# Two-block transformer step on one core: the first normalisation moved behind the transposes, column sums by transposes, gates and two key products column by column, other slots for the loads

## The chip, the cores and the metric

One core of one Trainium2 chip runs one program on 256 tokens of width 1024. The metric is the device time of one execution in microseconds (us); the number that counts is the median of several runs. The engines are PE (TensorE, matmuls and transposes), DVE (VectorE), ACT (ScalarE), POOL (GpSimd) and SP (SyncE, which here only issues the weight loads). Each executes its own instructions in the order in which they stand in its queue.

## The reference, cut to what matters

Two blocks follow each other. The first one is all that the change touches:

```python
mod = silu(c) @ w_ada + b_ada                      # 6 vectors of 1024: sh_m, sc_m, gt_m, sh_f, sc_f, gt_f
h = rmsnorm(x, norm_mix_g) * (1 + sc_m) + sh_m
q, k, v, f_logit, u = split(h @ w_in)              # 512, 512, 512, 8, 512 columns
log_f = log_sigmoid(f_logit + b_fgate)             # forget gates, 8 heads; F = cumsum(log_f)
x = x + gt_m * (concat(forgetting_attention(q, k, v, log_f), multiscale_pool(u)) @ w_out)
h = rmsnorm(x, norm_ffn_g) * (1 + sc_f) + sh_f
x = x + gt_f * hierarchical_moe(h)                 # 32 experts, 2 per token, 96 MB of weights
x = rmsnorm(x, norm_final_g)
# second block: stick-breaking attention, HGRN2, merge, square-ReLU MLP
```

## The kernel before, in words

All weights are streamed from HBM in tiles of 1 MB (128 x 2048 floats) by SP, in one fixed order, each into a numbered slot of SBUF (`Stream`, from L26; the issue is L51). SP issues a load when the slot's last tenant has been read, and a load that waits holds back all loads behind it. In the first part there are 11 slots (0 to 10). The order and the slots stand in the table `plan`: `a0` to `a7` are the eight tiles of `w_ada` that give sh_m and sc_m, `b` and `c` the other sixteen, `i0` and `i1` the keys' weights, `i2` and `i3` the values', `i4` to `i7` pairs of query and pool features, `o0` to `o3` `w_out`. Behind them come the 96 expert tiles (`w_gu`, `w_dn`), whose slots are those of the list `slots` and five extra ones: 18 tiles can lie ready before the first is read.

Products with `w_in` are made in three passes: a half tile of weights is split into a rounded part `whi` (ACT, L70) and a remainder `wlo` (DVE, L71), the activations are split likewise into `hT` and `hL`, and `mmx` (L140 to L142) issues hi x hi, hi x lo and lo x hi. `next2` takes the next split half and has the following ones split ahead, three halves at most.

The front runs in this order. (1) The rows of x get their norm: squares on ACT (L251), `r1` on DVE (L252, L243 to L245), and both halves are scaled (L257 on DVE, L259 on ACT). (2) PE transposes the scaled rows (L274) to eight columns of features, `xT[0..7]`. (3) For each column d of 128 features, `ada_first` makes the modulation: eight products of tile `a_d` with silu(c) (L292) in four strips of PSUM, a copy to `mr` (ACT, L294), and two one-column matmuls with ones that add the strips up (L298); it makes the products of column d+1 before the sums of column d. DVE adds the bias (L299) and forms A1 (L359). (4) `evac_split` turns column d into `hT` and `hL`: even columns DVE (L351), ACT (L352), POOL (L353), odd columns ACT (L344), DVE (L345, L346). (5) With all columns done: 24 small matmuls for the forget gates (`pf`), their log-sigmoid on ACT (L378 to L382) and cumulative sum on DVE (L383 to L389), then four key products (`feat`, 24 matmuls each), the values, and in turn queries, attention scores and pooling; single steps of the other modulation tiles (`some`, L311 to L325) lie between. `w_out`, the router and the experts follow, and then the second block.

Of the kernel before, what the change touches and what calls it, by code (L numbers as in the profile page):

```python
# [14 lines left out]
OP = mybir.AluOpType  # L15
# [102 lines left out]
LOOK, LOOK3 = 2, 3  # L118
SOME = (1, 1, 1, 1, 1, 3, 2, 2)
# [3 lines left out]
def body(tc, nc, ctx, a, out):  # L123
# [56 lines left out]
    st.slots.update({i: (ring if i < 4 else ring2, f"w{i}") for i in range(11)})  # L180

    st.slots.update({15: (hp_, "hT"), 16: (hp_, "hL")})
    plan = "a0-7 0-7 i0-4 0-4 b0-3 5-8 i5 9 b4 10 b5 5 i6 6 b6-7 7-8 c0 0 i7 1 c1-2 2-3 o0 8 c3 10 c4 5 c5 7 o1 0 c6 4 c7 2 o2 3 o3 10"
    src = {"a": (a["w_ada"][0], 0), "b": (a["w_ada"][1], 0), "c": (a["w_ada"][2], 0), "i": (a["w_in"], 1), "o": (a["w_out"], 1)}

    def span(x):
        lo, _, hi = x.partition("-")
        return range(int(lo), int(hi or lo) + 1)

    plan = plan.split()  # L190
    for what, where in zip(plan[::2], plan[1::2]):
        w, split = src[what[0]]
        for i, slot in zip(span(what[1:]), span(where)):
            st.add(w[i], split, slot)
# [60 lines left out]
    def scale_rows(dst, src, r, t):  # L255
        if t == 0:
            V.tensor_scalar(dst[:, t], src[:, t], r[:, t:t + 1], None, op0=OP.mult)  # L257
        else:
            S.activation(dst[:, t], src[:, t], AF.Copy, scale=r[:, t:t + 1])  # L259

    xn = cp.tile([128, 2, 1024], F32, name="xn")
    r1 = q1.tile([128, 2], F32, name="r1")
    rms_scale(r1, xt, q1, xn)
    for t in range(2):
        scale_rows(xn, xt, r1, t)
# [12 lines left out]
    xT = transposed(ps, "a", xn)  # L278
# [4 lines left out]
    def ada_first():  # L283

        last = None
        for d in range(9):
            if d < 8:
                w = st.next()
                pa = ps.tile([128, 512], F32, name="pa", tag="m", bufs=2)
                for k in (0, 2, 4, 6, 1, 3, 5, 7):  # L290
                    j = 32 * (k // 2)
                    mm(pa[j:j + 32, 0:256], cs[:, k, :], w[:, 256 * k:256 * k + 256], start=(k % 2 == 0), stop=(k % 2 == 1))  # L292
                mr = q1.tile([128, 256], F32, name="mr", bufs=2)
                S.activation(mr, pa[:, 0:256], AF.Copy)  # L294
            if last:
                pl, ml = last
                for j in range(2):
                    mm(pl[:, 256 + j:257 + j], ml[:, 128 * j:128 * j + 128], ones, start=True, stop=True)  # L298
                V.tensor_tensor(modT[:, 0:2, d - 1], pl[:, 256:258], vec[:, V_BA + d - 1:V_BA + 16:8], op=OP.add)  # L299
                yield  # L300
            last = pa, mr
# [27 lines left out]
    def mod(m):  # L329
        return modT[:, m]  # L330
# [72 lines left out]
    for i in range(4):  # L403
        feat(st.next2(), kT[:, i])
# [40 lines left out]
    scr = q1.tile([128, 2048], F32, name="scr", tag="scr")  # L445
# [251 lines left out]
    slots = [9, 15, 16, 5, 7, 2, 1, 0, 3, 6, 4, 8, 10]  # L697
# [1084 lines left out]
```

## Time and profile before

| what | us |
|---|---|
| three runs | 750.92, 746.55, 751.06 (median 750.92) |
| the profiled execution, its own time | 746.88 |
| its span, first to last instruction | 745.1 |
| mean granted TensorE clock in it | 0.967 |
| PE busy | 681.0 (91% of the span) |
| DVE, ACT, POOL busy | 398.4, 303.8, 139.9 |

Busy shares are means over parts with different limits: to about 151 us the front with its attention and router, from there to about 350 us the experts, then the second block. Starts are in us from the span's start. A matmul's row shows its whole passage through the array; how often one is started is read from the distance of the starts.

### The profile page before, as it was taken

The numbers are of one execution on the slowest core, as the hardware profiler recorded it, in microseconds if no ns is written. First come the engines' busy times: TensorE is split into PE (matmuls) and PEld (weight loads), VectorE is DVE, ScalarE is ACT, GpSimd is POOL, SyncE is SP. The second block draws the span as 40 slices with busy tenths as digits, with TensorE's granted clock in tenths as the row PEclk, the third lists the DMA queues.
The fourth block names the chain that finished last, engine by engine and source line by source line (L and its number), as shares of the span: only waits on it lengthen the run. The fifth ranks groups of instructions, "written<-read, shape, count | busy, mean of one in ns | idle before, by whom it ended". The sixth has DMA issues, their size and how long they took to land.

```text
span 745.1 us, 12246 instructions
## 1 busy us (share of the span) xinstructions
PE 681.0 (91%) x4953; PEld 525.2 (70%) x4953; DVE 398.4 (53%) x661; ACT 303.8 (41%) x531; POOL 139.9 (19%) x137
## 2 busy tenths in 40 slices
PE   3899999889799877877899999999999999999995
PEld 2598867644244313311799999999989998989885
DVE  2676896522122112011888877777867654545545
ACT  3544534321011001001585566586456654535433
POOL 0102521000000000000604342222413530503201
PEclk9999999999889889789999999999999999999998
DMA  9999499999999999999664333355446655455511
GB/s 362 418 420 408 192 408 420 419 384 421 419 420 420 421 421 421 421 422 421 253 211 169 131 114 113 115 191 205 170 170 206 218 175 219 172 186 207 173 58 56
DMA packets 29726, 207.70 MB, mean 279 GB/s; under 512 B 3553, under 2 KB 3937, under 8 KB 4706
## 3 DMA queue, kind: packets, MB, share of 16 engines
q1 hardware_dynamic: 29520, 206.35, 70.3%
q8 instruction: 41, 0.67, 0.4%
q10 hardware_dynamic: 146, 0.53, 0.2%
q14 instruction: 19, 0.16, 0.1%
HBM read 205.81 MB, written 1.05 MB: 278 GB/s over the span
## 4 chain that ended last, share of the span: by engine, by line
PE 52%; DMA 16%; DVE 3%; ACT 1%; issue 1%; DVEq 0%; ACTq 0%; SPq 0%
DMA w<-in_w_gu 11%; PE pp L140 9%; PE pp L141 9%; PE pp L142 9%; DMA w<-in_w_dn 5%; PE fy L142 4%; PE fy L141 4%; PE fy L140 4%; PE pB L1265 2%; PE y L847 1%; PE pv L140 1%; PE pv L141 1%; PE pv L142 1%; PE acc L141 1%; PE acc L140 1%; PE acc L142 1%
## 5 line engine op out<-in xcount | busy, mean ns | idle before, releaser
L71 DVE TENSOR_TENSOR wlo<-w,whi 128x1024 fp32r<-128x1024 f32 x144 | 182.0, 1267 | 98.0 <-ACT whi L70 97.7
L70 ACT ACTIVATE whi<-w 128x1024 fp32r<-128x1024 f32 x146 | 153.4, 1054 | 78.5 <-PE fy L142 39.7
L141 PE MATMUL pp<-hL,whi 128*128 128x256 f32 x368 | 102.9, 280 | 2.6 <-DVE hL L876 2.6
L140 PE MATMUL pp<-hT,whi 128*128 128x256 f32 x368 | 105.1, 286 | 0.0
L142 PE MATMUL pp<-hT,wlo 128*128 128x256 f32 x368 | 103.1, 280 | 0.5 <-DVE wlo L71 0.5
L930 PE MATMUL pgu<-w,hg 128*32 128x512 f32 x512 | 70.3, 665 | 20.3 <-DMA w<-in_w_gu 20.2
L140 PEld LDWEIGHTS pp<-hT,whi 128*128 128x128 f32 x368 | 70.0, 190 | 3.5 <-issue 2.4
L141 PEld LDWEIGHTS pp<-hL,whi 128*128 128x128 f32 x368 | 69.7, 189 | 2.8 <-POOL wlo L71 2.7
L140 PE MATMUL pp<-nH,whi 128*128 128x256 f32 x256 | 71.5, 279 | 0.0
L141 PE MATMUL pp<-nL,whi 128*128 128x256 f32 x256 | 71.3, 279 | 0.0
L142 PE MATMUL pp<-nH,wlo 128*128 128x256 f32 x256 | 71.3, 279 | 0.0
L142 PEld LDWEIGHTS pp<-hT,wlo 128*128 128x128 f32 x368 | 70.0, 190 | 0.7 <-DVE wlo L71 0.7
L930 PEld LDWEIGHTS pgu<-w,hg 128*32 128x32 f32 x512 | 14.2, 113 | 71.4 <-issue 46.8
L1544 POOL TENSOR_TENSOR aL<-rs,aH 128x256 fp32r<-128x256 f32 x32 | 46.1, 1442 | 86.7 <-ACT aH L1543 80.8
L934 DVE TENSOR_TENSOR act<-pgu,act 128x256 f32<-128x256 f32 x8 | 3.4, 425 | 104.4 <-ACT act L933 104.4
L933 ACT ACTIVATE act<-pgu 128x256 f32<-128x256 f32 x8 | 3.1, 383 | 127.8 <-PE pgu L930 127.8
L142 PEld LDWEIGHTS pp<-nH,wlo 128*128 128x128 f32 x256 | 48.6, 190 | 0.0
L141 PE MATMUL fy<-wlo,aH 128*128 128x512 f32 x124 | 48.2, 389 | 0.0
L142 PE MATMUL fy<-whi,aL 128*128 128x512 f32 x124 | 48.2, 389 | 0.0
L140 PE MATMUL fy<-whi,aH 128*128 128x512 f32 x124 | 48.2, 389 | 0.0
L141 PEld LDWEIGHTS pp<-nL,whi 128*128 128x128 f32 x256 | 48.1, 188 | 0.1
L140 PEld LDWEIGHTS pp<-nH,whi 128*128 128x128 f32 x256 | 48.1, 188 | 0.1
(430 smaller groups left out, 1286.7 us busy)
## 6 DMA issues: line engine op xcount, KB each, us to landing
w<-in_w_gu SPq DMA_DIRECT2D x64, 1024.0 KB, 19.8
w<-in_w_dn SPq DMA_DIRECT2D x32, 1024.0 KB, 19.8
w<-in_w_ff SPq DMA_DIRECT2D x32, 1024.0 KB, 4.8
w<-in_w_in SPq DMA_DIRECT2D x30, 1024.0 KB, 5.9
w<-in_w_ada SPq DMA_DIRECT2D x24, 1024.0 KB, 12.5
w<-in_w_out SPq DMA_DIRECT2D x8, 1024.0 KB, 4.8
w<-in_w_o SPq DMA_DIRECT2D x4, 1024.0 KB, 4.8
xt<-in_x SPq DMA_DIRECT2D x1, 1024.0 KB, 4.8
```

Source lines behind the costliest of these rows:

```text
L70: nc.scalar.activation(hi, w, AF.Copy)
L71: low = lambda e, lo=lo, w=w, hi=hi: e.tensor_tensor(lo, w, hi.bitcast(F32), op=OP.subtract)
L140: mm(out_, l[0], r[0], start=start, stop=False)
L141: mm(out_, l[0], r[1], start=False, stop=False)
L142: mm(out_, l[1], r[0], start=False, stop=stop)
L847: mm(pacc[t][h], pw[g][:, 128 * t:128 * t + 128], o, start=False, stop=(g == 7))
L930: mm(pgu[32 * j:32 * j + 32], hg[g][:, k, 32 * j:32 * j + 32], w[:, 512 * j:512 * j + 512], start=(k == 0), stop=(k == 7))
L933: S.activation(act, pgu[:, 0:256], AF.Silu)
L934: V.tensor_tensor(act, pgu[:, 256:512], act, op=OP.mult)
L1265: mm(p[:, 4 * t + h], kt[:, h, 128 * t:128 * t + 128], qo[:, h, n * t:n * t + n], start=True, stop=True)
L1544: G.tensor_tensor(aL[:, f], s, aH[:, f].bitcast(F32), op=OP.subtract)
```

## The change

Seven edits, all in the front, and the slots of later loads:

1. The rows are transposed raw (`transposed(ps, "a", xt)`), before the norm. The factor `r1` is brought across all partitions by a matmul: a diagonal matrix `dg1` (DVE, two instructions) times a matrix of ones, copied out as `rb1` (ACT). The scaling of the rows (L257, L259) is gone.
2. The strip sums of a column come from two transposes and a DVE reduction over every 32nd column of the result; the bias is added in an instruction of its own.
3. A column leaves PSUM in one form for all d: DVE multiplies by A1 and `rb1` (`evt`), ACT adds the shift and rounds (`hT`), DVE forms the remainder (`hL`). POOL has no part in it.
4. The sums of column d now stand in the program before the products of column d+1.
5. From column 3 on, between the products and the sums of column d, PE makes the matmuls of column d-2 for two key products and for the gates (nine); tile `i0` is split before that, behind column 2.
6. The splits of `i1` come after column 7; the copies of the first two key products (`kT`) come behind the gates' log-sigmoid.
7. `plan` loads `i0` between `a2` and `a3`, `i1` behind `a7`, and gives other slots; so do `slots` and `RING`, from which the second block's weights are loaded.

```diff
+RING = (4, 5, 7, 1)
...
-    plan = "a0-7 0-7 i0-4 0-4 b0-3 5-8 i5 9 b4 10 b5 5 i6 6 b6-7 7-8 c0 0 i7 1 c1-2 2-3 o0 8 c3 10 c4 5 c5 7 o1 0 c6 4 c7 2 o2 3 o3 10"
+    plan = """a0:0 a1:1 a2:2 i0:3 a3:4 a4:5 a5:6 a6:7 a7:8 i1:9 i2:10 i3:0 i4:1 b0:2 b1:3 b2:4 b3:5 i5:6 b4:7 b5:8 i6:9 b6:10 b7:2
+        c0:3 i7:0 c1:4 c2:5 o0:1 c3:7 c4:6 c5:8 o1:10 c6:9 c7:2 o2:0 o3:3"""
-    plan = plan.split()
...
-        if t == 0:
-            V.tensor_scalar(dst[:, t], src[:, t], r[:, t:t + 1], None, op0=OP.mult)
-        else:
-            S.activation(dst[:, t], src[:, t], AF.Copy, scale=r[:, t:t + 1])
-    r1 = q1.tile([128, 2], F32, name="r1")
-    rms_scale(r1, xt, q1, xn)
-    for t in range(2):
-        scale_rows(xn, xt, r1, t)
+    scr = q1.tile([128, 2048], F32, name="scr", tag="scr")
+    full = scr[:, 0:128]
+    G.memset(full, 1.0)
...
-    xT = transposed(ps, "a", xn)
+    xT = transposed(ps, "a", xt)
+    r1 = q1.tile([128, 2], F32, name="r1")
+    rms_scale(r1, xt, q1, xn)
+    dg1, rb1 = scr[:, 128:384], scr[:, 384:640]
+    for t in range(2):
+        V.tensor_scalar(dg1[:, 128 * t:128 * t + 128], ident, r1[:, t:t + 1], None, op0=OP.mult)
+    def row_scales():
+        p = ps.tile([128, 256], F32, name="prb1", tag="s", bufs=2)
+        mm(p, full, dg1, start=True, stop=True)
+        S.activation(rb1, p, AF.Copy)
-    def ada_first():
-        last = None
-        for d in range(9):
-            if d < 8:
-                w = st.next()
-                pa = ps.tile([128, 512], F32, name="pa", tag="m", bufs=2)
-                for k in (0, 2, 4, 6, 1, 3, 5, 7):
-                    j = 32 * (k // 2)
-                    mm(pa[j:j + 32, 0:256], cs[:, k, :], w[:, 256 * k:256 * k + 256], start=(k % 2 == 0), stop=(k % 2 == 1))
-                mr = q1.tile([128, 256], F32, name="mr", bufs=2)
-                S.activation(mr, pa[:, 0:256], AF.Copy)
-            if last:
-                pl, ml = last
-                for j in range(2):
-                    mm(pl[:, 256 + j:257 + j], ml[:, 128 * j:128 * j + 128], ones, start=True, stop=True)
-                V.tensor_tensor(modT[:, 0:2, d - 1], pl[:, 256:258], vec[:, V_BA + d - 1:V_BA + 16:8], op=OP.add)
-                yield
-            last = pa, mr
+    pas = {}
+    def ada_products(d):
+        w = st.next()
+        pa = ps.tile([128, 512], F32, name="pa", tag="m", bufs=2)
+        for k in (0, 2, 4, 6, 1, 3, 5, 7):
+            j = 32 * (k // 2)
+            mm(pa[j:j + 32, 0:256], cs[:, k, :], w[:, 256 * k:256 * k + 256], start=(k % 2 == 0), stop=(k % 2 == 1))
+        mr = q1.tile([128, 256], F32, name="mr", bufs=2)
+        S.activation(mr, pa[:, 0:256], AF.Copy)
+        pas[d] = pa, mr
+    def ada_sums(d):
+        pa, mr = pas.pop(d)
+        p = pa[:, 256:512].rearrange("p (j c) -> p j c", j=2)
+        for j in range(2):
+            nc.tensor.transpose(p[:, j], mr[:, 128 * j:128 * j + 128], ident)
+        m = modT[:, 0:2, d]
+        V.tensor_reduce(m, p[:, :, 0:128:32], axis=AX.X, op=OP.add)
+        V.tensor_tensor(m, m, vec[:, V_BA + d:V_BA + 16:8], op=OP.add)
+        V.scalar_tensor_tensor(A1[:, d:d + 1], mod(1)[:, d:d + 1], 1.0, vec[:, V_GM + d:V_GM + d + 1], op0=OP.add, op1=OP.mult)
+        e = q1.tile([128, 256], F32, name="evt", bufs=3)
+        V.scalar_tensor_tensor(e, xT[d], A1[:, d:d + 1], rb1, op0=OP.mult, op1=OP.mult)
+        sh = mod(0)[:, d:d + 1]
+        S.activation(hT[:, d], e, AF.Identity, bias=sh)
+        V.scalar_tensor_tensor(hL[:, d], e, sh, hT[:, d].bitcast(F32), op0=OP.add, op1=OP.subtract)
...
-    for d, _ in enumerate(ada_first()):
-        V.scalar_tensor_tensor(A1[:, d:d + 1], mod(1)[:, d:d + 1], 1.0, vec[:, V_GM + d:V_GM + d + 1], op0=OP.add, op1=OP.mult)
-        evac_split(q1, xT[d], hT[:, d], hL[:, d], A1[:, d:d + 1], mod(0)[:, d:d + 1], v=d % 2)
-    st.split_to(LOOK)
+    pf, early = [], []
+    def gate_column(k):
+        if not pf:
+            pf.append(ps.tile([128, 256], F32, name="pf", tag="s", bufs=2))
+        mmx(pf[0][0:8], (wfh[:, k], wfl[:, k]), (hT[:, k], hL[:, k]), start=(k == 0), stop=(k == 7))
+    def key_column(k):
+        if not early:
+            early.extend((ps.tile([128, 256], F32, name="pp", tag=tag, bufs=n), st.next2(False)) for tag, n in (("a", 4), ("s", 2)))
+        for p, w in early:
+            mmx(p, sub(w, slice(None), slice(128 * k, 128 * k + 128)), (hT[:, k], hL[:, k]), start=(k == 0), stop=(k == 7))
+    ada_products(0)
+    row_scales()
+    ada_sums(0)
+    for d in (1, 2):
+        ada_products(d)
+        ada_sums(d)
+    gate_column(0)
+    st.split_to(2)
+    key_column(0)
+    for d in range(3, 8):
+        ada_products(d)
+        key_column(d - 2)
+        gate_column(d - 2)
+        ada_sums(d)
+    for k in (6, 7):
+        key_column(k)
+        gate_column(k)
+    st.split_to(1)
     nc.sync.dma_start(wpl, a["w_pool"])
     nc.sync.dma_start(wr, a["w_r"])
...
-    pf = ps.tile([128, 256], F32, name="pf", tag="a", bufs=4)
-    for k in range(8):
-        mmx(pf[0:8], (wfh[:, k], wfl[:, k]), (hT[:, k], hL[:, k]), start=(k == 0), stop=(k == 7))
-    S.activation(fz, pf[0:8], AF.Identity, bias=vec[0:8, V_BF:V_BF + 1])
+    S.activation(fz, pf[0][0:8], AF.Identity, bias=vec[0:8, V_BF:V_BF + 1])
...
     for i in range(4):
-        feat(st.next2(), kT[:, i])
+        if i < 2:
+            S.activation(kT[:, i], early[i][0], AF.Copy)
+        else:
+            feat(st.next2(), kT[:, i])
...
-    slots = [9, 15, 16, 5, 7, 2, 1, 0, 3, 6, 4, 8, 10]
+    slots = [4, 15, 16, 5, 7, 1, 6, 8, 9, 10, 2, 0, 3]
-            st.add(a[name][i], True, (2, 1, 0, 3)[n % 4])
+            st.add(a[name][i], True, RING[n % 4])
```

In ACT's queue before, around columns 1 to 3 (`mr` is the copy of a column's strip products, `evt` and `hT` the scaled and the rounded column; numbers count the buffers):

```order
L294 ACTIVATE mr_216<-pa_207 128x256
L344 ACTIVATE evt_222<-ptr_143,modT_163,A1_168 128x256
L294 ACTIVATE mr_237<-pa_228 128x256
L352 ACTIVATE hT_169<-evt_243 128x256
L294 ACTIVATE mr_258<-pa_249 128x256
```

The same place now, from the copy of column 1 to `hT` of column 3 (`whi_248` and `whi_252` are the two halves of tile `i0`):

```order
L295 ACTIVATE mr_209<-pa_200 128x256
L311 ACTIVATE hT_171<-evt_216,modT_165 128x256
L295 ACTIVATE mr_231<-pa_222 128x256
L311 ACTIVATE hT_171<-evt_238,modT_165 128x256
L70 ACTIVATE whi_248<-w3_246 128x1024
L70 ACTIVATE whi_252<-w3_246 128x1024
L295 ACTIVATE mr_275<-pa_266 128x256
L311 ACTIVATE hT_171<-evt_291,modT_165 128x256
```

Before, the copy of column d+1 (`mr_216` is column 2) stood ahead of the work on column d (`evt_222` is column 1); now it stands behind `hT` of column d. The two splits of `i0` stood behind column 7 and now stand between columns 2 and 3.

PE's queue now, from the products of column 2 to those of column 3 (`pf` gates, `pp_256` and `pp_257` the two key products):

```order
L293 MATMUL pa_222<-w2_220,cs_115 32x256 x8
L303 MATMUL pa_222<-ident_75,mr_231 128x128 x2
L141 MATMUL pf_242<-hT_171,wfh_166 8x256
L142 MATMUL pf_242<-hL_172,wfh_166 8x256
L143 MATMUL pf_242<-hT_171,wfl_167 8x256
L141 MATMUL pp_256<-hT_171,whi_248 128x256
L142 MATMUL pp_256<-hL_172,whi_248 128x256
L143 MATMUL pp_256<-hT_171,wlo_249 128x256
L141 MATMUL pp_257<-hT_171,whi_252 128x256
L142 MATMUL pp_257<-hL_172,whi_252 128x256
L143 MATMUL pp_257<-hT_171,wlo_253 128x256
L293 MATMUL pa_266<-w4_264,cs_115 32x256 x8
```

The first nine matmuls of gates and keys stand ahead of the products of column 3, and the last of them reads `wlo_253`, the remainder of the second half of `i0`.

SP's queue before, around the first load of `w_out` (w8 is slot 8):

```order
L51 DMA w2_1094<-in_w_ada 128x2048
L51 DMA w3_1101<-in_w_ada 128x2048
L51 DMA w8_1103<-in_w_out 128x2048
L51 DMA w10_1177<-in_w_ada 128x2048
L51 DMA w5_1242<-in_w_ada 128x2048
```

The same loads now:

```order
L51 DMA w4_1106<-in_w_ada 128x2048
L51 DMA w5_1113<-in_w_ada 128x2048
L51 DMA w1_1115<-in_w_out 128x2048
L51 DMA w7_1189<-in_w_ada 128x2048
L51 DMA w6_1254<-in_w_ada 128x2048
```

The order of the tiles is the same; `o0` goes to slot 1, whose tenant is `i4`, and no longer to slot 8, whose tenant was `b7`.

## Rows read from the trace of the kernel before

**Rows 1.** The page's second part: the span in 40 slices of 18.6 us, granted PE clock in tenths, DMA throughput.

```profile
PEclk9999999999889889789999999999999999999998
GB/s 362 418 420 408 192 408 420 419 384 421 419 420 420 421 421 421 421 422 421 253 211 169 131 114 113 115 191 205 170 170 206 218 175 219 172 186 207 173 58 56
```

**Rows 2.** Table by stretches: start:end, length, busy us and (instructions) of each engine, then granted clock, DMA share, GB/s.

```profile
72.00:88.00 16.00, 16.00 (x148) 12.63 (x150) 13.93 (x30) 7.81 (x26) 9.43 (x16) 1.00 0.36 140
152.00:160.00 8.00, 6.61 (x62) 1.88 (x54) 0.76 (x2) 2.50 (x5) 0.00 (x0) 1.00 0.86 322
196.00:200.00 4.00, 2.10 (x20) 0.39 (x12) 0.53 (x2) 0.38 (x1) 0.00 (x0) 1.00 1.02 422
200.00:212.00 12.00, 9.75 (x24) 5.16 (x25) 0.32 (x1) 1.19 (x2) 0.00 (x0) 0.57 1.01 418
```

**Rows 3.** SP's queue in order of time (start, length of the issue): the loads around the first `w_out` tile, and the first loads issued after the experts' matmuls have begun.

```profile
58.41 0.85 SPq L51 DMA_DIRECT2D w<-in_w_ada  x2
83.27 0.33 SPq L51 DMA_DIRECT2D w<-in_w_out  x1
...
153.12 1.46 SPq L51 DMA_DIRECT2D w<-in_w_gu  x2
```

**Rows 4.** Whom SP waited for in the whole span: us in total, times, longest.

```profile
SPq L51 <- DVE xn L313: 48.4, 10, 23.9
```

**Rows 5.** The chain that ended last, its two last long pieces in the experts (start, length).

```profile
308.76 21.05 DMA w<-in_w_gu
329.87 19.91 DMA w<-in_w_dn
```

**Rows 6.** Whom PE waited for from 30 to 150 us, the longest entry of eight (us in total, times, longest).

```profile
PE pgb L538 <- DVE evt L349: 1.6, 1, 1.6
```

**Rows 7.** PE in order of time: the first matmul of the key products, the 49th (the third product's first), the 96th, and what follows.

```profile
33.59 0.28 PE L140 MATMUL pp<-hT,whi 128*128 128x256 f32 x1
...
40.00 0.28 PE L140 MATMUL pp<-hT,whi 128*128 128x256 f32 x1
...
45.35 0.28 PE L142 MATMUL pp<-hT,wlo 128*128 128x256 f32 x1
45.56 0.64 PE L311 MATMUL pa<-w,cs 128*32 128x256 f32 x8
```

**Rows 8.** The opening in order of time, all engines: start, length, engine, line, what, [idle before <- releaser].

```profile
10.84 0.16 DVE L245 SCALAR_TENSOR_TENSOR r<-isu,isw 128x2 f32<-128x2 f32 x1
11.84 3.86 PE L274 MATMUL ptr<-ident,xn 128*128 128x128 f32 x16 [11.84 <-DVE xn L257]
...
18.11 0.38 ACT L294 ACTIVATE mr<-pa 128x256 f32<-128x256 f32 x1 [0.48 <-PE pa L292]
18.68 0.16 DVE L299 TENSOR_TENSOR modT<-pa,vec 128x2 f32<-128x2 f32 x1 [6.53 <-PE pa L298]
18.90 1.07 PE L292 MATMUL pa<-w,cs 128*32 128x256 f32 x16 [0.32 <-DVE modT L299]
19.07 0.55 DVE L351 TENSOR_SCALAR evt<-ptr,A,modT 128x256 f32<-128x256 f32 x1
19.65 0.42 ACT L352 ACTIVATE hT<-evt 128x256 fp32r<-128x256 f32 x1 [1.16 <-DVE evt L351]
```

**Rows 9.** Groups by line and shape in the first 150 us: busy us and mean ns of one, then idle before.

```profile
L71 DVE TENSOR_TENSOR wlo<-w,whi 128x1024 fp32r<-128x1024 f32 x24 | 30.1, 1263 | 19.5 <-ACT whi L70 19.4
L351 DVE TENSOR_SCALAR evt<-ptr,A,modT 128x256 f32<-128x256 f32 x4 | 2.2, 544 | 0.2
L346 DVE TENSOR_TENSOR hL<-evt,hT 128x256 fp32r<-128x256 f32 x4 | 1.7, 426 | 0.1
L435 DVE SCALAR_TENSOR_TENSOR up<-s,up 128x240 f32<-128x240 f32 x2 | 0.8, 402 | 0.0
L735 DVE TENSOR_REDUCE ab<-ao 128x8 f32<-128x64 f32 x1 | 0.2, 220 | 0.0
L486 DVE TENSOR_SCALAR scr<-scr,mx 128x128 f32<-128x128 f32 x8 | 3.3, 418 | 0.3
L160 DVE TENSOR_SCALAR lt<-jp 128x128 f32<-128x128 int32 x1 | 0.2, 221 | 0.0
L70 ACT ACTIVATE whi<-w 128x1024 fp32r<-128x1024 f32 x24 | 25.1, 1055 | 4.5 <-PE pv L142 4.5
```

**Rows 10.** PE in order of time: four transposes, and eight.

```profile
88.67 0.66 PE L324 MATMUL pa<-ident,mr 128*128 128x128 f32 x4
...
353.82 1.09 PE L865 MATMUL ptr<-ident,xt 128*128 128x128 f32 x8
```

**Rows 11.** The gates' chain on ACT and DVE, first and last pieces, in order of time.

```profile
33.85 0.46 ACT L378 ACTIVATE fz<-pf,vec 8x256 f32<-8x256 f32 x1
35.24 0.51 ACT L382 ACTIVATE fa<-fa,ones 8x256 f32<-8x256 f32 x1
...
35.78 0.41 DVE L383 SCALAR_TENSOR_TENSOR fz<-fz,fa 8x256 f32<-8x256 f32 x1 [0.22 <-ACT fa L382]
38.85 2.36 DVE L71 TENSOR_TENSOR wlo<-w,whi 128x1024 fp32r<-128x1024 f32 x2
```

**Rows 12.** PE in order of time, after a wait at the second block's start.

```profile
368.07 0.28 PE L141 MATMUL pp<-hL,whi 128*128 128x256 f32 x1
...
368.78 0.41 PE L142 MATMUL pp<-hT,wlo 128*128 128x256 f32 x1
```

More of the change, by code (lines that the diff above doesn't have):

```diff
@@ L179, in body @@
     st.split_pool = wp
-    st.slots.update({i: (ring if i < 4 else ring2, f"w{i}") for i in range(11)})
+    st.slots.update({i: (ring if i in RING else ring2, f"w{i}") for i in range(11)})
     st.slots.update({15: (hp_, "hT"), 16: (hp_, "hL")})
-    plan = "a0-7 0-7 i0-4 0-4 b0-3 5-8 i5 9 b4 10 b5 5 i6 6 b6-7 7-8 c0 0 i7 1 c1-2 2-3 o0 8 c3 10 c4 5 c5 7 o1 0 c6 4 c7 2 o2 3 o3 10"
+    plan = """a0:0 a1:1 a2:2 i0:3 a3:4 a4:5 a5:6 a6:7 a7:8 i1:9 i2:10 i3:0 i4:1 b0:2 b1:3 b2:4 b3:5 i5:6 b4:7 b5:8 i6:9 b6:10 b7:2
+        c0:3 i7:0 c1:4 c2:5 o0:1 c3:7 c4:6 c5:8 o1:10 c6:9 c7:2 o2:0 o3:3"""
     src = {"a": (a["w_ada"][0], 0), "b": (a["w_ada"][1], 0), "c": (a["w_ada"][2], 0), "i": (a["w_in"], 1), "o": (a["w_out"], 1)}
-    def span(x):
-        lo, _, hi = x.partition("-")
-        return range(int(lo), int(hi or lo) + 1)
-    plan = plan.split()
-    for what, where in zip(plan[::2], plan[1::2]):
+    for what in plan.split():
+        what, slot = what.split(":")
         w, split = src[what[0]]
-        for i, slot in zip(span(what[1:]), span(where)):
-            st.add(w[i], split, slot)
+        st.add(w[int(what[1:])], split, int(slot))
     ones = cp.tile([128, 1], F32, name="ones")
@@ L253, in rms_scale @@
         inv_sqrt(dst, ss, pool, 2)
-    def scale_rows(dst, src, r, t):
-        if t == 0:
-            V.tensor_scalar(dst[:, t], src[:, t], r[:, t:t + 1], None, op0=OP.mult)
-        else:
-            S.activation(dst[:, t], src[:, t], AF.Copy, scale=r[:, t:t + 1])
     xn = cp.tile([128, 2, 1024], F32, name="xn")
-    r1 = q1.tile([128, 2], F32, name="r1")
-    rms_scale(r1, xt, q1, xn)
-    for t in range(2):
-        scale_rows(xn, xt, r1, t)
+    scr = q1.tile([128, 2048], F32, name="scr", tag="scr")
+    full = scr[:, 0:128]
+    G.memset(full, 1.0)
     def transposed(ps, tag, src):
@@ L441, in pool_out @@
         evac_split(q1, p, catH[:, i], catL[:, i], vec[:, V_PS + g:V_PS + g + 1])
-    scr = q1.tile([128, 2048], F32, name="scr", tag="scr")
     scr2 = q1.tile([128, 1040], F32, name="scr2", tag="scr2")
```

## The prediction, made before the changed kernel ran

> **What bounds the kernel now.** I read the page's slices first. From the second slice to the nineteenth (18.6 to 354 us) the loads run at 420 GB/s, with one hole in the fifth slice (192 GB/s) [rows 1]. The table by stretches gives its size: 140 GB/s from 72 to 88 us, so 16 x (1 - 140/420) = 10.7 us without loads; and a second hole, 322 GB/s from 152 to 160 us, 8 x (1 - 322/420) = 1.9 us [rows 2]. SP's queue says why there is a first one: after 58.41 no load is issued until 83.27, and that load is the first of `w_out` [rows 3]; SP's waits name its 23.9 us wait: L313, the DVE instruction that reads the tile `b7` in slot 8 [rows 4]. The second hole ends with the first load into a slot that an expert has freed, at 153.12 [rows 3]: all 18 expert tiles that fit had landed by then.
>
> That decides what the first hole is worth. Of 96 expert tiles 78 come after 153.12, and the chain shows the last one landing at 329.87 + 19.91 = 349.8 [rows 5]: 196.7 us for 78, 2.52 us each, the rate of a tile at 420 GB/s. So the end of the experts is the first expert read plus a fixed 196.7 us, and loads that come earlier in the front only wait in full slots. What does count is when the front's computation ends. There PE is the bound: from 30 to 150 us its longest wait is 1.6 us and none is for a load [rows 6]. A shift of PE at 45 us should therefore arrive at 153 us and at the end, undiminished. All the rest is to find that shift.
>
> **The change part by part.** The measuring point is the last matmul of the four key products, at 45.35 in the trace, behind which the kernel's order is as before [rows 7].
>
> *Opening.* The raw transposes no longer wait for the norm (they started at 11.84 for L257 [rows 8]). This buys nothing by itself: the first column now needs `rb1`. `r1` is ready at 10.84 + 0.16 = 11.0 [rows 8]. Two 128x128 DVE products with a factor per row: between 0.22 (L160) and 0.42 us (L486) each [rows 9], I take 0.3, to 11.6. The matmul with ones is 256 columns wide, as two transposes are; four take 0.66 [rows 10], so 0.4 to 0.66, I take 0.5, to 12.1. The copy like `mr`, 0.38 [rows 8], to 12.5.
>
> *One column.* The chain before is seen at 18.11: copy, sums, bias, `evt`, `hT`, 0.03 to 0.1 us between dependent steps [rows 8]. The new one, from copy to copy: `mr` 0.38 and 0.06; two transposes 0.40 (a first passage 0.27, a second start 0.13 later [rows 10]) and 0.10; the reduction, not seen in this form: 0.22 for the nearest, L735 [rows 9]; bias and A1 0.16 each [rows 8], three gaps 0.04; `evt`, between 0.40 (L435) and 0.54 (L351) [rows 9], I take 0.47; `hT` 0.42 [rows 8], two gaps 0.03. Sum 2.5 us. Because ACT's queue now holds the copy of column d+1 behind `hT` of column d, this is the period; before, the copy stood ahead. With the cheap ends it is 2.4, with the dear ones (reduction 0.41, like L486) 2.8. PE's share of a column, products 1.07 [rows 8], nine matmuls at 0.114 (that is (45.35 - 40.00)/47 [rows 7]) and the transposes, is also 2.5, and a tile lands every 2.5 us, so neither shortens it. The `hL` that leaves POOL costs DVE 0.43 [rows 9], beside this chain. First `hT`: sums from 12.1, `evt` done at 13.7, `hT` at 14.1; then column 1 at 16.6, column 2 at 19.1.
>
> *The split in the middle.* ACT now makes both halves of `i0`, 2 x 1.055 [rows 9], to 21.2, DVE both remainders at 1.23, the second to 22.7. PE waits for it at the first key matmuls, and the products of column 3 stand behind them: 22.8, though tile `a3` landed long before. Products to 23.9, nine matmuls to 24.9, sums to `hT` 2.1: column 3 at 27.0, and four periods later column 7 at 37.1; `hL` 37.6, the last nine matmuls to 38.6. The same work was done at 40.00 [rows 7], so PE is 1.4 us ahead here.
>
> *What comes late next.* The other splits are now behind column 7. First half of `i1`: ACT to 38.2, DVE to 39.4; the third key product runs 39.4 to 42.0. Then ACT makes the gates' chain, 1.9 us (33.85 to 35.75 [rows 11]), 38.8 to 40.7, two `kT` copies to 41.5, and only then the second half's `whi`, to 42.6. DVE's gate chain takes 3.07 us (35.78 to 38.85 [rows 11]), 40.7 to 43.8, and only then `wlo`, to 45.0. In the kernel before, two key products of PE work covered these chains; they are now done beforehand, and the cover is gone. So the fourth key product gets its third matmul at 45.1 and ends 21 x 0.114 later, at 47.5 instead of 45.35: 2.2 us late. With cheap columns +0.9, with dear ones +4.2.
>
> *TensorE's clock.* From about 17.5 to 22.8 PE has only nine small matmuls. In the trace 2.1 us of PE work in the 4 us from 196 were followed by 12 us at a mean granted clock of 0.57 [rows 2], that is mostly 1.2 GHz; and at 368 us, after another wait, matmuls already running went from 0.12 to 0.21 us apart [rows 12]. At that level a column costs PE 2.1 + 9 x 0.21 + 0.8 = 4.8 us instead of 2.5. The bounds are no column and two and a half (12 us), 0 to +6; I take two thirds of a column, +1.5.
>
> *Loads.* The new slots let `o0` go after `i4` and fill the first hole; by the above this is worth 0, hidden by the full slots before 153.12. `b0`, needed at 47.5, has the same tiles ahead of it as before, when 45.56 was early enough [rows 7]. `slots` and `RING` change names, not numbers, of slots: 0.
>
> *Sum.* 2.2 + 1.5 = +3.7. The profiled execution took 746.9 us by itself (span 745.1 and 1.8 around it): 750.6. The median shown, 750.92, is 4.0 above that execution; of four times two lie near 746.7 and two near 751. For a median I add half of the 4.0: **752.6 us**. A measurement of this kernel can tell about 1% (7.5 us) from no change.
>
> **The rivals.** *A, the column stage keeps pace with the loads.* For it: PE had idle time before 30 us, and `a7` is the ninth tile now; 1.2 MB of small inputs and nine tiles of 1.05 are 10.7 MB, 6.7 of them in the first slice, the rest at 418 GB/s [rows 1], so it lands at 28.0. If columns followed that, column 7 would be at 28.0 + 1.07 + 1.05 + 2.1 = 32.2, the key matmuls done at 33.7, the gate chains at 38.9, `wlo` at 40.1, the fourth product at 42.6: 2.8 us early, 744.1 (746.1 as a median). Against it: ACT's order, which ties copies to `hT`, and the split in the middle. 0.22.
>
> *B, the hole was the loss.* If the expert loads set the end whatever the experts have read, filling both holes gives 746.9 - 10.7 - 1.9 = 734.3. For it: the chain lies on loads from 308.76 [rows 5]. Against it: the hole at 152 with slots full. 0.05.
>
> *C, slower: PE stays at 1.2 GHz through the column stage.* Then five columns cost 2.3 us more each and the first two 0.8, 13.1 in all: 746.9 + 2.2 + 13.1 = 762.2. It decides for over 1% from about two and a half slow columns on. For it: the sixteen opening transposes took 3.86 us, 0.24 each, against 0.13 later [rows 8, 10]: PE was busy and still at the lower level. Against it: products and nine matmuls fill PE at either level, and the columns before the change ran at 1.07 for their products right behind those transposes [rows 8]. 0.14.
> The Trainium skill (TensorE: Matmul & The Clock Gate, Part 4: PE-mode transpose) says that transposes do not count as activity that lifts the clock. The opening's 0.24 us agrees; by that rule the column stage, which trades matmuls for transposes, is slower to reach the full clock, which is rival C.
>
> **How the numbers follow.** My forecast (a shift of 0.9 to about 7 us, PE waiting behind the splits) has 0.59, A 0.22, B 0.05, C 0.14. Range 745 to 760: at the low end A as a median less 1, at the high end 746.9 + 4.2 + 6 + part of the 4.0; it leaves out B and most of C. Faster by over 1%: B and a little of A, 0.06. Slower by over 1%: C, 0.14. Within 1%: the rest, 0.80.
>
> **What would show it.** In the profile after: `hT` every 2.5 us with the copy right behind; PE idle before column 3 with DVE `wlo` named; the products of column 3 at about 22.8; gates and two key products done at 38.6; a PE wait for `wlo` in the fourth key product, up to 45; no hole at 72 us but a larger one before the first expert slot comes free, and that at 153.1 plus the shift, with the last tile 196.7 us behind. I am wrong if the products of columns 3 to 7 start as their tiles land, or if the shift at the key products does not reach 153 us.

## The result, and the profile after

| | us |
|---|---|
| changed kernel, median of 7 runs | 754.74 (754.13 to 755.09) |
| kernel before, beside it, median of 7 | 747.11 (746.12 to 751.06) |
| ratio | 1.0094, interval [1.0078, 1.0110] |
| profiled execution, its span, mean clock | 755.09, 753.4, 0.960 |

The change costs 0.9%. The forecast was 752.6, in a range of 745 to 760 and most likely within 1% of before: that held, and so did the direction. But the sum behind it was +3.7, and the profiled executions differ by 8.2.

The page's slices, granted clock and DMA throughput (answering to [rows 1]):

```profile
PEclk9799999999979989898999999999999999999998
...
GB/s 361 419 421 421 358 291 422 181 372 422 421 419 421 420 420 422 421 421 421 311 193 181 168 114 112 113 169 177 201 179 194 202 194 195 197 171 202 187 57 56
```

The second slice (18.6 to 37 us) now has a lower clock, and the hole in the loads (time in which they run below their 420 GB/s) has moved: the fifth slice has 358 GB/s (192 before), the sixth 291, the eighth 181. The table by stretches says how much (columns as in [rows 2]):

```profile
72.00:84.00 12.00, 12.00 (x109) 10.17 (x107) 9.72 (x23) 6.29 (x21) 5.90 (x11) 1.00 1.00 409
84.00:100.00 16.00, 16.00 (x151) 12.68 (x151) 12.88 (x31) 9.09 (x23) 10.37 (x18) 1.00 0.69 249
124.00:140.00 16.00, 16.00 (x91) 13.16 (x90) 8.64 (x14) 5.50 (x9) 0.00 (x0) 1.00 0.90 359
140.00:148.00 8.00, 7.09 (x54) 6.16 (x52) 2.87 (x7) 2.68 (x8) 0.00 (x0) 1.00 0.12 18
148.00:164.00 16.00, 14.07 (x110) 7.52 (x113) 7.13 (x42) 5.80 (x11) 0.00 (x0) 1.00 0.86 344
```

ACT in order of time, from `rb1` to the last column (answering to [rows 8]); lengths and idle time as there:

```profile
12.63 0.39 ACT L280 ACTIVATE scr<-prb 128x256 f32<-128x256 f32 x1 [1.03 <-PE prb L279]
14.12 0.51 ACT L311 ACTIVATE hT<-evt,modT 128x256 fp32r<-128x256 f32 x1 [1.10 <-DVE evt L309]
...
19.35 0.51 ACT L311 ACTIVATE hT<-evt,modT 128x256 fp32r<-128x256 f32 x1 [1.96 <-DVE evt L309]
19.76 1.99 ACT L70 ACTIVATE whi<-w 128x1024 fp32r<-128x1024 f32 x2
25.83 0.38 ACT L295 ACTIVATE mr<-pa 128x256 f32<-128x256 f32 x1 [4.07 <-PE pa L293]
29.28 0.51 ACT L311 ACTIVATE hT<-evt,modT 128x256 fp32r<-128x256 f32 x1 [3.07 <-DVE evt L309]
...
39.25 0.51 ACT L311 ACTIVATE hT<-evt,modT 128x256 fp32r<-128x256 f32 x1 [1.71 <-DVE evt L309]
```

The four periods from 29.28 to 39.25 (2.49 each) are those of the forecast; the first `hT` starts at 14.12 and ends at about 14.6, where the forecast had its end at 14.1. Between columns 2 and 3 lie 9.9 us. PE in order of time, from the sums of column 1 on, shows what filled them, and the wait in the fourth product (answering to [rows 7]):

```profile
14.95 0.44 PE L303 MATMUL pa<-ident,mr 128*128 128x128 f32 x2 [1.14 <-ACT mr L295]
...
17.44 0.69 PE L303 MATMUL pa<-ident,mr 128*128 128x128 f32 x2 [1.05 <-ACT mr L295]
...
20.86 0.58 PE L141 MATMUL pp<-hT,whi 128*128 128x256 f32 x1 [2.09 <-ACT whi L70]
22.12 0.58 PE L143 MATMUL pp<-hT,wlo 128*128 128x256 f32 x1 [0.46 <-DVE wlo L71]
...
23.76 1.94 PE L293 MATMUL pa<-w,cs 128*32 128x256 f32 x16
...
47.91 0.44 PE L143 MATMUL pp<-hT,wlo 128*128 128x256 f32 x1 [2.36 <-DVE wlo L71]
...
52.03 0.28 PE L143 MATMUL pp<-hT,wlo 128*128 128x256 f32 x1
52.23 0.64 PE L322 MATMUL pa<-w,cs 128*32 128x256 f32 x8
```

The products of column 3 take 1.94 us instead of 1.07, and the 22 matmuls from 47.91 to 52.03 are 0.20 apart in the mean instead of 0.114. The granted clock of the same kernel says why (PE busy, granted clock, DMA share, GB/s):

```profile
16.00:17.00 1.00, 0.39 (x8) 1.00 0.97 410
17.00:18.00 1.00, 0.56 (x3) 0.69 1.03 434
18.00:20.00 2.00, 0.77 (x4) 0.50 1.02 430
20.00:24.00 4.00, 2.56 (x10) 0.50 1.01 424
24.00:28.00 4.00, 4.00 (x29) 0.55 1.02 422
28.00:32.00 4.00, 4.00 (x48) 1.00 1.01 403
...
48.00:52.00 4.00, 4.00 (x21) 0.57 1.01 418
```

0.50 is 1.2 GHz. Both falls follow idle time. The first comes between 17 and 18 us, behind two waits of 1.14 and 1.05 us for the copies of columns 1 and 2; the wait of 2.09 us for the split of `i0` begins when the clock is already low. The second follows the 2.36 us of waiting for `wlo`. The point where the order is as before, 45.56 in [rows 7], comes at 52.23, 6.7 us late.

### The profile page after: what moved, and what is told of

Its sections match the earlier page's. It is cut to its first block, busy times and chain, and to the rows that moved or that the text cites. A ratio compares the mean times of both kernels' runs of the same rounds, so it can differ in the third digit from the quotient of the medians.

```text
span 753.4 us, 12229 instructions
## 1 busy us (share of the span) xinstructions
PE 685.1 (91%) x4939; PEld 528.7 (70%) x4939; DVE 402.2 (53%) x674; ACT 302.1 (40%) x531; POOL 137.6 (18%) x134
## 3 DMA queue, kind: packets, MB, share of 16 engines
HBM read 205.81 MB, written 1.05 MB: 275 GB/s over the span
## 4 chain that ended last, share of the span: by engine, by line
PE 50%; DMA 18%; DVE 3%; ACT 1%; issue 1%; DVEq 0%; SPq 0%; ACTq 0%
DMA w<-in_w_gu 11%; PE pp L141 9%; PE pp L142 9%; PE pp L143 9%; DMA w<-in_w_dn 7%; PE fy L141 4%; PE fy L142 4%; PE fy L143 4%; PE pB L1303 2%; PE pv L141 1%; PE pv L143 1%; PE pv L142 1%; PE y L885 1%; PE acc L142 1%; PE acc L141 1%; PE acc L143 1%
## 5 line engine op out<-in xcount | busy, mean ns | idle before, releaser
L141 PE MATMUL pp<-hT,whi 128*128 128x256 f32 x368 | 107.7, 293 | 3.0 <-ACT whi L70 2.3
L143 PE MATMUL pp<-hT,wlo 128*128 128x256 f32 x368 | 104.9, 285 | 3.2 <-DVE wlo L71 3.1
L142 PE MATMUL pp<-hL,whi 128*128 128x256 f32 x368 | 104.5, 284 | 2.7 <-DVE hL L914 2.6
L968 PE MATMUL pgu<-w,hg 128*32 128x512 f32 x512 | 67.8, 646 | 23.5 <-DMA w<-in_w_gu 23.5
L142 PEld LDWEIGHTS pp<-hL,whi 128*128 128x128 f32 x368 | 71.4, 194 | 3.1 <-POOL wlo L71 2.7
```

The lines of the kernel that those rows point to most:

```text
L141: mm(out_, l[0], r[0], start=start, stop=False)
L142: mm(out_, l[0], r[1], start=False, stop=False)
L143: mm(out_, l[1], r[0], start=False, stop=stop)
L968: mm(pgu[32 * j:32 * j + 32], hg[g][:, k, 32 * j:32 * j + 32], w[:, 512 * j:512 * j + 512], start=(k == 0), stop=(k == 7))
```

## The experiments

Each kernel's time is the median of 4 to 12 runs beside the kernel before (747.0 to 748.4 in these batches). "Point" is the start of the modulation step behind the key products (45.56 before, 52.23 after); no value stands where the edit leaves it or moves that step.

| kernel | us | ratio to before, interval | point |
|---|---|---|---|
| changed kernel | 754.74 | 1.0094 [1.0078, 1.0110] | 52.23 |
| before, new loads only | 753.60 | 1.0083 [1.0066, 1.0100] | 52.04 |
| the same, waiting time filled | 748.91 | 1.0019 [1.0002, 1.0036] | 47.36 |
| after, both halves of i1 split together | 748.97 | 1.0021 [1.0005, 1.0038] | 47.15 |
| after, filled ahead of product 4 | 751.65 | 1.0059 [1.0047, 1.0071] | 51.03 |
| after, large fillers early | 758.06 | 1.0146 [1.0132, 1.0161] | 56.32 |
| after, small fillers in the waits | 752.53 | 1.0060 [1.0040, 1.0080] | 51.44 |
| after, splits of i0 spread | 745.51 | 0.9974 [0.9957, 0.9992] | 43.64 |
| after, gathers filled | 755.46 | 1.0096 [1.0072, 1.0121] | – |
| spread and all fillers | 746.64 | 0.9979 [0.9966, 0.9993] | 43.99 |
| before, gathers filled | 747.12 | 0.9999 [0.9982, 1.0016] | – |
| spread, front fillers, b0 later | 745.57 | 0.9979 [0.9964, 0.9994] | – |
| spread, b0 later | 746.49 | 0.9995 [0.9981, 1.0009] | – |

**The loads alone.** The kernel before, with only the new `plan`, `slots` and `RING`.

> The kernel before with nothing of the change but its load plan: the order with i0 between a2 and a3, the new slots, RING. Theory 1 (the end follows PE in the front, loads that come earlier only wait in full slots): no change against before, -0.5 to +0.5 us, the hole at 72 us gone and one of about 12 us ahead of the first expert slot that comes free. Rival (the hole was a loss, or the new slots delay the loads): -10 us, or most of the +7.6 that the whole change cost.

Measured 753.6: theory 1 was wrong, the rival's size came. But not by the slots. PE in order of time at column 6:

```profile
27.96 1.93 PE L289 MATMUL pa<-w,cs 128*32 128x256 f32 x16 [1.64 <-DMA w<-in_w_ada]
```

and the stretch behind it (PE busy, granted clock, DMA share, GB/s):

```profile
28.00:40.00 12.00, 11.68 (x69) 0.50 1.02 420
```

With `i0` in front, `a6` lands one tile later; the old front, which runs a column in 1.9 us, waits 1.64 us for it, and the clock falls to 1.2 GHz for more than 12 us. So this run charges the new order with a clock that the changed kernel, whose columns are slower, does not lose there. To tell the wait from the clock, 24 small matmuls were put into the wait:

```diff
+                for _ in range(24 if d == 6 else 0):
+                    mm(pa[64:96, 384:512], identb[:, 0:32], onesb, start=True, stop=True)
```

> The kernel before with only the new order of loads and slots (as in the first experiment), and 24 small bf16 matmuls (128 columns each, their result unused) ahead of column 6's products, where TensorE waited 1.64 us for w_ada's tile and the granted clock fell to 0.50 from 28 to 40 us. Theory 1 (the wait for the tile costs some 2.5 us, the rest of the 6.4 at the key products is the clock that fell in that wait): the clock stays at 1.00, products of column 6 take 1.07 instead of 1.93, the gates and key products run at a spacing of 0.12 throughout, they end 2.5 to 3 us later than in the kernel before, and the time is 749 to 750. Rival (the clock falls for another reason than this wait, or the new slots cost the time): the time stays at 752 to 754.

Column 6 again (the first three of its sixteen rows lie among the last fillers), column 7, and the same stretch:

```profile
28.14 1.03 PE L291 MATMUL pa<-w,cs 128*32 128x256 f32 x13
...
30.09 1.07 PE L291 MATMUL pa<-w,cs 128*32 128x256 f32 x16 [0.39 <-DVE modT L298]
```

```profile
28.00:40.00 12.00, 11.04 (x111) 1.00 1.02 419
```

748.91: theory 1, with a smaller price for the late tile. The same loads with idle matmuls are 4.7 us faster; the late tile costs 1.8 at the point (47.36; 2.5 to 3 were expected), the clock the other 4.7 (from 52.04).

**The late split.**

```diff
-    st.split_to(1)
+    st.split_to(2)
     nc.sync.dma_start(wpl, a["w_pool"])
```

> The changed kernel with split_to(2) in place of split_to(1) behind the columns: both halves of i1 are split ahead of the gates' chain. Theory 1 (the fourth key product waits for wlo queued behind the gates' chain, 2.4 us, and the clock falls in that wait, 1.5 us): the fourth product ends at 47.5 instead of 52.1, the next part waits up to 48.7 for the first half of i2, so about -4.1 us against the changed kernel, +3.5 against before. Rival (the front is late for other reasons, and this wait is covered later on): -1 us or less.

748.97, 5.8 below the changed kernel, more than the 4.1 expected: the wait of 2.36 us in the fourth product is gone and with it the low clock behind it, and the next part does not wait; the point moves 5.1 us forward. The same clock without the order, by six fp32 matmuls ahead of the fourth product:

```diff
+        for _ in range(fill):
+            mm(p, ident, xt[:, 0, 0:256], start=True, stop=True)
...
+            feat(st.next2(), kT[:, i], fill=6 if i == 3 else 0)
```

> The changed kernel with six idle matmuls ahead of the fourth key product, which stands waiting there for wlo until 47.9. Theory 1: the fourth product runs at 0.117 instead of 0.21 us per matmul and ends 1.5 us earlier; the end about 1.5 us earlier. Rival (only the wait counts, or the clock falls anyway): 0.

Its wait for `wlo` is 0.3 us and its matmuls are 0.114 apart; the point moves 1.2 forward, the time 3.1. The profiled executions differ by 1.2 as well (753.93), so the clock's part is shown; what else is in the 3.1 of the medians stays open.

**The column stage.** First with fp32 fillers of 256 columns between 13 and 21 us:

```diff
+        if d in (1, 2):
+            filler(pa[:, 256:512], 2)
...
+        if d == 2:
+            filler(pa[:, 0:256], 5)
```

> The changed kernel with nine idle matmuls on PE (identity times raw rows, 128x256, into PSUM that is overwritten afterwards): two each ahead of the transposes of columns 1 and 2, five behind those of column 2. They do nothing but keep PE at work between 13 and 21 us. Theory 1 (PE's clock falls there, and column 3 runs at 1.2 GHz): products of column 3 start at 23.8 as before and take 1.07 instead of 1.94 us, nine matmuls 1.03 instead of 1.9, columns 3 to 7 come 2 to 2.7 us earlier, and the end about 2.5 us earlier. Rival (the split of i0 alone sets column 3): 0, or slower by what the nine matmuls take (4 us).

758.06, a miss: the fillers stood in the path (the gates' first matmul went from 17.78 to 21.43), and the clock fell behind them all the same. Then small bf16 ones, as long as the waits:

```diff
+            mm(pf[0][64:96, 0:128], identb[:, 0:32], onesb, start=True, stop=True)
...
         ada_products(d)
+        filler(14)
         ada_sums(d)
     gate_column(0)
+    filler(30)
```

> The changed kernel with small bf16 matmuls (result unused) put where TensorE waits in the first columns: 14 behind the products of columns 1 and 2 each, 30 behind the gates' first column, about as long as the waits there (1.1, 1.05 and 2.1 us), so that they push nothing. Theory 1 (the clock that fell in these waits costs 2.6 us at column 3): the granted clock stays at 1.00 up to 28 us, products(3) take 1.07 instead of 1.94, nine key matmuls go at 0.12, the fourth key product ends some 2.5 us earlier, and the time is 752. Rival (column 3 is held by the splits on VectorE and ScalarE, and the low clock lies in their shade): clock at 1.00 but the time within 1 us of 754.7.

752.53, the time of theory 1, but only part of its mechanism: the clock held until about 23 us (0.99 from 20 to 24, then 0.58), the products of column 3 took 1.32, and the point moved 0.8, not 2.5. What is left is the split itself, taken apart next:

```diff
+    ada_products(2)
+    st.split_to(1)
+    ada_sums(2)
+    st.split_to(2)
     gate_column(0)
-    key_column(0)
     for d in range(3, 8):
         ada_products(d)
-        key_column(d - 2)
         gate_column(d - 2)
+        if d > 3:
+            key_column(d - 4)
         ada_sums(d)
+    for k in (4, 5):
+        key_column(k)
...
-    st.split_to(1)
+    st.split_to(2)
```

> The changed kernel with the same loads, in which the two halves of i0 are no longer split together between columns 2 and 3: one half's split is queued ahead of column 2's copy, the other behind it, the key columns follow four columns later instead of two, and both halves of i1 are split behind the columns. Theory 1 (the column stage lost its time at the splits of i0, which hold column 3 for 7 us, and after that each column only takes its 2.5 us): column 3's products start when their tile is there, some 3 us sooner (20.5 instead of 23.8) and at the full clock; hT(7) at 34 to 35 us instead of 39.3, the fourth key product ends at 42 to 44 us instead of 52.0, and the time is 744 to 747. Rival (the columns are held by their own chain and by the low clock wherever the splits stand): hT(7) stays at 37 or later, and the time is that of the version with two splits, 749, or more.

```profile
20.64 0.51 ACT L311 ACTIVATE hT<-evt,modT 128x256 fp32r<-128x256 f32 x1 [2.28 <-DVE evt L309]
21.05 1.04 ACT L70 ACTIVATE whi<-w 128x1024 fp32r<-128x1024 f32 x1
22.00 0.36 ACT L295 ACTIVATE mr<-pa 128x256 f32<-128x256 f32 x1
24.37 0.51 ACT L311 ACTIVATE hT<-evt,modT 128x256 fp32r<-128x256 f32 x1 [2.01 <-DVE evt L309]
...
35.41 0.51 ACT L311 ACTIVATE hT<-evt,modT 128x256 fp32r<-128x256 f32 x1 [1.71 <-DVE evt L309]
```

Column 3 comes at 24.37 instead of 29.28, column 7 at 35.41 instead of 39.25, the point at 43.64, and the time is 745.51: theory 1 held, with the last `hT` 0.4 later than it said; its profiled execution, 749.45, was its longest. The clock still fell, one column later: 0.58 from 22 to 24 us, and the products of column 4 took 1.94. This is the changed kernel's idea with its two waits for splits gone, and it is 0.3% faster than the kernel before, by an interval that just leaves out 1.

**What holds the end.** Do the gathers' low clocks, seen in some executions, cost time?

```diff
             pg = pm.tile([128, 4, 128], F32, name="pg", tag="t", bufs=4)
+            for _ in range(16 if b == 0 and g < 2 else 0):
+                mm(pg[64:96, 0], onesb[:, 0:32], ltb, start=True, stop=True)
```

> The changed kernel with 16 small bf16 matmuls (result unused) ahead of the first matmul of the first two expert groups' gathers, where TensorE waits 1.1 and 0.85 us for VectorE's P. Theory 1 (each of these gathers runs in some executions at 1.2 GHz for its first 5 us, 5.4 instead of 3.8 us, because TensorE idled just before; in the changed kernel's profile the second did): both gathers take 3.8 us, and the time is 752.5 to 753.5, 1.2 to 2.2 below the changed kernel. Rival (the clock there has another reason, or the experts' loads set the pace and the 1.6 us are hidden): 754 to 755.

PE at the two gathers, and whom it waited for most from 140 to 385 us (us, times, longest):

```profile
155.87 3.81 PE L850 MATMUL pg<-P,xn 128*128 128x128 f32 x32
...
169.41 3.84 PE L850 MATMUL pg<-P,xn 128*128 128x128 f32 x32
```

```profile
PE pgu L970 <- DMA w<-in_w_gu: 27.3, 22, 1.5
```

Both gathers take 3.8 us and nothing is gained (755.46): in the experts PE waits 22 times for `w_gu`, 27.3 us in all, 23.5 in the changed kernel. But this profiled execution had lost the clock elsewhere, so that its first gather came 1.7 us later than the changed kernel's (154.18):

```profile
119.53 1.78 PE L576 MATMUL pgb<-ident,modT 128*128 128x128 f32 x8 [1.63 <-DVE evt L360]
```

These eight took 1.09 us in the changed kernel, and the granted clock is 0.50 from 120 to 122 us here, 1.00 there. A cleaner pair is the second gather of the changed kernel and of the new loads alone, which reach it 0.1 us apart:

```profile
167.64 5.42 PE L848 MATMUL pg<-P,xn 128*128 128x128 f32 x32 [0.85 <-DVE P L839]
```

```profile
167.75 3.84 PE L807 MATMUL pg<-P,xn 128*128 128x128 f32 x32 [0.85 <-DVE P L798]
```

One is 1.6 us longer, and the executions took 755.09 and 755.08: the rival's reading, that the loads set the pace there. The same fillers in the kernel before:

> The kernel before with the same 16 matmuls ahead of the first two gathers. Theory 1: its profile has both gathers at the full clock (746.9), its slower executions (up to 751) have one or both at the lower clock; the median falls to 746 to 747 and the spread shrinks to under 2 us. Rival (the spread has other reasons): median and spread stay at 747.5 and 5 us.

747.12, still 746.61 to 749.77: the rival; the cause of these executions' spread stays open. Only one execution is profiled, and a short one. A fall of the clock behind the wait ahead of `pgb`, as above, is a candidate: of the fourteen profiled executions two have it, that with the gathers filled and that of the spread splits (749.45, its kernel's longest). Spread splits with all fillers:

> The version whose splits of i0 are spread over columns 2 and 3 (745.5 measured), with small bf16 matmuls (result unused) in the waits of the first columns (14, 14, 18, 14, behind the products of columns 1 and 2, the gates' first column, and the gates' second) and the 16 ahead of the first two gathers. Theory 1 (clock): the granted clock stays at 1.00 from 12 to 28 us, where it was 0.79 and 0.78, the fourth key product ends 1 to 1.5 us earlier than 43.6, both gathers take 3.8 us instead of 5.4, and the time is 742 to 744.5, below both kernels. Rival (behind 45 us the loads hold it, so that what is won in front is lost at the first expert slots): 745 to 746.

746.64, 0.2% below the kernel before, but short of the 742 to 744.5 of theory 1 and above the rival's 745 to 746. The clock was 1.00 from 10 to 50 us and column 7 came 1.2 us earlier than without fillers, but PE then waited for a tile:

```profile
43.99 0.64 PE L322 MATMUL pa<-w,cs 128*32 128x256 f32 x8 [1.52 <-DMA w<-in_w_ada]
```

The front had caught up with its transfers. So that tile was taken up later, in both runs without the gathers' fillers, once with those of the front and once without:

```diff
-    some(1)
     for i in range(2):
         pv = [ps.tile([128, 256], F32, name="pv", tag="a", bufs=4) for t in range(2)]
...
-            some(i + kh < 2)
+            some(1)
```

> The version with spread splits and small matmuls in the waits of the first columns, without those ahead of the gathers, and with w_ada's tile b0 taken up behind the first half of the value products instead of ahead of them, since TensorE waited 1.5 us for its transfer there. Theory 1 (the end follows TensorE's place when the phase's buffers come free at about 140 us): TensorE stands 2.5 to 3 us ahead of the kernel before from 48 to 140 us, the holes in the transfers sum to 14 us or less by 200 us (15.4 in the kernel before), and the time is 743.5 to 745.5. Rival (from here the transfers hold the middle, so that a faster front is taken back before 140 us): a wait for another tile replaces this one, and the time stays at 746 to 747.

> The version with spread splits, no added matmuls, and only b0 moved behind the first half of the value products. Theory 1: TensorE did not wait for b0 in that version (its front is slower by the clock), so nothing changes: 745 to 746. Rival (b0's place matters for when its buffer comes free and so for the later transfers): off by more than 1 us either way.

745.57 and 746.49; the intervals of these two and of the spread version overlap, and neither which is best nor theory 1 of the second can be told. The first missed what it was to show by little (holes of 14.6 us for 14, 745.57 for 745.5). In the first PE stands 3.0 us ahead of the kernel before at the last key matmul (42.31 against 45.35) and 2.4 at 99 us, a little less than said, and from 44 to 124 us its transfers have next to no hole (0.1 us by the sum below). They have it later (columns as in [rows 2]):

```profile
72.00:84.00 12.00, 12.00 (x110) 9.82 (x109) 11.22 (x28) 6.15 (x18) 7.03 (x15) 1.00 1.01 420
84.00:100.00 16.00, 16.00 (x156) 12.03 (x155) 13.45 (x25) 8.32 (x24) 6.29 (x11) 1.00 1.01 418
124.00:140.00 16.00, 15.09 (x92) 12.53 (x91) 7.77 (x20) 4.78 (x12) 0.00 (x0) 1.00 0.45 162
140.00:148.00 8.00, 6.06 (x38) 4.22 (x37) 5.71 (x35) 1.85 (x4) 0.00 (x0) 1.00 1.01 423
```

124 to 140 us: 16 x (1 - 162/420) = 9.8 us of hole. Sum the holes in this way from 0 to 200 us (stretches 0, 44, 72, 100, 124, 152, 164, 200) and set them beside the profiled execution's own time:

| kernel | hole to 124 us | to 200 us | time | time less holes |
|---|---|---|---|---|
| before | 13.7 | 15.4 | 746.9 | 731.5 |
| changed | 11.1 | 23.9 | 755.1 | 731.2 |
| loads only | 12.1 | 23.2 | 755.1 | 731.9 |
| loads only, filled | 6.2 | 18.6 | 748.7 | 730.1 |
| i1 split together | 6.0 | 19.0 | 749.0 | 730.0 |
| large fillers | 15.7 | 28.2 | 759.6 | 731.4 |
| ahead of product 4 filled | 9.8 | 22.4 | 753.9 | 731.5 |
| small fillers in the waits | 10.4 | 23.1 | 753.8 | 730.7 |
| gathers filled | 12.0 | 25.4 | 755.5 | 730.1 |
| before, gathers filled | 13.7 | 15.4 | 746.7 | 731.3 |
| spread and all fillers | 3.9 | 15.6 | 745.6 | 730.0 |
| splits spread | 3.6 | 17.0 | 749.5 | 732.5 |
| spread, front fillers, b0 later | 2.7 | 14.6 | 744.0 | 729.4 |
| spread, b0 later | 2.8 | 14.7 | 746.3 | 731.6 |

Times span 15.6 us, times less holes 3.1. The time is some 731 us plus the holes, and where in the front a hole lies does not matter: what counts is when the first expert has been read. Differences of 2 us or so this sum does not explain: the last two rows have the same holes and lie 2.3 apart.

## Why the prediction was right or wrong

**Holes worth nothing: right.** The hole at 72 us went (409 GB/s from 72 to 84). Most of it returned at 124 to 148, ahead of the first expert's slot, as the forecast said it would; that 16 x (1 - 249/420) = 6.5 us return at 84 to 100 already it did not say. From the first load into a freed slot to the last expert tile the forecast had 196.7 us. SP's issue of that load in the changed kernel (answering to [rows 3, 5]):

```profile
161.52 0.80 SPq L51 DMA_DIRECT2D w<-in_w_gu  x2
```

and the chain's last expert tile:

```profile
338.02 19.89 DMA w<-in_w_dn
```

338.02 + 19.89 - 161.52 = 196.4; in the version with front fillers and `b0` later 329.19 + 19.89 - 152.41 = 196.7. Rival B falls with that version: its first hole, priced there at 10.7 us, is gone, and the profiled execution took 744.0, where 746.9 - 10.7 = 736.2 was due.

**The opening and the column's period: nearly right.** `rb1` done at 13.0 (12.5 said), first `hT` done at 14.6 (14.1), so 0.5 us late from the start; period 2.49 (2.5). Rival A did not come: with the splits spread the period is still 2.49 from column 4 on and column 7 comes at 35.4, not 32.2. That this version's time (745.5) is near rival A's (746.1) is not rival A's pace.

**The split in the middle: right place, too small.** Products of column 3 at 23.76 (22.8 said), `hT` of column 3 done at 29.8 (27.0), of column 7 at 39.8 (37.1), the third matmul of the fourth key product at 47.91 (45.1): 2.8 us more, and all of it is there when column 3's nine matmuls end at 27.68 (24.9). The opening makes 0.5 of it, the way from there to the products of column 3 another 0.5, and the rest is the low clock, next.

**The cover that is gone: right.** A PE wait for `wlo` of 2.36 us in the fourth product, named as such; splitting both halves together takes it away and is worth 5.8 us with the clock that goes with it.

**TensorE's clock: the term that was mis-sized.** +1.5 was taken, for column 3. Seen: 0.87 in its products, 1.0 in the nine matmuls behind them (25.63 to 27.68, 2.05 instead of 1.0), and (52.03 - 47.91) - 21 x 0.114 = 1.7 in the fourth product, 3.6 in all. The fall in the wait of the fourth product was not foreseen, though the wait was. With the 2.8 us that column 3 and the splits are later, two thirds of them this same clock, that is 2.8 + 1.7 - 1.5 = 3.0, the difference between 49.0, where the sum had the fourth product's end, and 52.03. Rival C did not come: the clock was 1.00 from 28 to 40 us, through columns 4 to 7. Of the opening's transposes, on which it leaned, the rows of before do not agree with each other: 0.24 us each, but a granted clock of 1.00 from 12 to 16 us; which level they ran at stays open.

**The shift arrives undiminished: nearly.** PE is 6.7 us late at the point and still 6.7 at the first gather (154.18 against 147.49). But the first load into a freed slot is 161.52 - 153.12 = 8.4 late. What SP waited for from 150 to 163 us:

```profile
SPq L51 <- DMA grow<-in_gain: 12.1, 1, 12.1
```

The profile names the landing of the small row `grow`, issued at 158.04, 3.5 us before the load; in the kernel before it was issued at 151.34, 1.8 before. In the changed kernel five tiles issued from 146.8 on were still landing when it was issued. That this wait makes the other 1.7 us was not tried.

**The median.** 2.0 us were added for the spread of the first three runs of before; its median turned out 747.11, so they were not due. They hid nearly half of what the sum lacked: 746.9 + 3.7 + 2.0 against 746.9 + 7.8. That the forecast lies 2.1 us from the median is in this part luck.

## What to carry to other kernels

Where buffers limit the loads, closing a hole only moves it: look for the instruction that frees the first buffer behind it, and shift that. When work is moved ahead to fill an engine's gaps, ask which chains it used to cover, and price not only the new wait but the clock behind it. An experiment that undoes or adds one part has its own waits: the new loads alone cost 6.5 us (753.60 against 747.14), 4.7 of them by a low clock behind column 6 that the whole change never had.

## What was not expected of the hardware

In the kernel before with the new loads, one wait of 1.64 us was followed by more than 12 us at 1.2 GHz, though TensorE was busy for 11.68 of the 12 from 28 to 40, with strip products and with gate matmuls whose result is 8 rows high; the spacing went to 0.12 about 1 us after the 128-row key products had begun at 39.83. The Trainium skill (TensorE: Matmul & The Clock Gate, Part 1: The HAM clock gate, on its oscillation in real kernels) has waits for transfers, there of 3 to 5 us, as a way to lose the clock; this trace agrees, with one of 1.64 us. That the clock can stay low through 12 us of such busy time, no row of before had shown. Idle bf16 matmuls of 128 columns, 0.06 us each, kept the clock at 1.00 where they fitted into the waits; fp32 ones of 256 columns, 0.23 to 0.28 us per pass, stood in the path in the column stage and cost 3.3 us (758.06 against 754.74), while in the longer wait ahead of the fourth product they gained 3.1.
